# Reordering the two router passages of a two-layer transformer kernel: shift logits, first expert weights, placements

## The chip, the cores and the metric

The kernel runs on one core of one Trainium2 chip, with all operands in fp32 in HBM. The metric is the device time of one execution in microseconds. TensorE's granted clock has two levels, 1.2 and 2.4 GHz; the profile writes them as 0.5 and 1.0.

## The reference, cut to what matters

Two layers run over 256 context rows and 256 latent rows of 1024 columns. Layer 0 mixes by grouped-query attention, layer 1 by an S5 scan with a gated linear unit (GLU) behind it. After each mixer comes a mixture of 32 experts in 4 groups. Layer 1 needs the latent rows alone.

```
m = split(silu(c) @ mod_w[i] + mod_b[i], 6)                # shift, scale, gate for mixer and experts
h = h + m[2] * mixer(modulate(rmsnorm(h, norm1_g), m[0], m[1]))
t = modulate(rmsnorm(h, norm2_g), m[3], m[4])              # = rmsnorm(h) * g * (1 + scale) + shift
g_logits = t @ w_group + b_group                           # 4 groups: the largest is taken
e_logits = (t @ w_router + b_router)[of that group]        # 8 experts: the best two are taken
y = sum over e of combine[:, e] * ((silu(t @ w_gate[e]) * (t @ w_up[e])) @ w_down[e])
h = h + m[5] * y
```

## The kernel before

The program order of each engine is written out by hand: the functions are generators, and the order in which they are stepped is the order of the instructions on every engine. An engine works its instructions off in that order, so one that waits holds up all that stand behind it.

**Layer 0's passage.** `attention` ends with `out(t)` for four row tiles: 16 steps of the output projection (L445), then a multiplication and an addition on VectorE (L449, L450). Between these steps TensorE also computes layer 1's modulation, one half of a 1024-column chunk at a time (`mod.half`, L142), and the router's preparation `prep(n, j)` of the tiles that are ready. The modulation weights (24 MB in loads of 1 MB) go through a ring of slots; a slot is loaded again once TensorE has read it. The ring is set by `c.use`: two slots of `own` (buffers named ring) and the five of `new` (buffers named more), while four slots of `own` hold the output projection. The last chunk's modulation stands behind `attention`, in `beside`.

**The router.** For a tile of 128 rows `prep` scales the rows (L647), takes the sum of squares, transposes them (L657), copies the result out of PSUM (L660, L662) and computes the logits (L691). The shift's share of the logits is the same for all rows of one kind and is made by `base(j)` once for each kind: on VectorE shift times router weights (L623), a sum (L625), then one small matmul (L629) and the bias (L631). `base` needs the router's weights `wr`, which `tables` loads on GpSimd's queue. `route` takes the groups and experts (L711 to L723), the exponentials for the combine weights (L726 to L728), the position of each row in its expert's list by a matmul (L732), and writes rows and weights into the lists by matmuls with one-hot matrices (`place`, L776).

**The experts.** In layer 0, `start` computes the row indices, gathers 128 rows for two experts at a time by indirect DMA (L909), and issues weights on GpSimd's queue; the loop `experts` transposes the gathered rows (L923), computes gate and up (L936), transposes (L947), multiplies by the down matrix (L957), and adds into the rows (L1001) two experts later. Expert e+4's weights take the slots of older ones. In layer 1 the rows of an expert are picked by one-hot matmuls (`open`, L859, for the first four experts; `quad`, L823, for the rest).

**Layer 1's passage.** `s5.glu(1, wg)` is the second column half of the GLU, 32 steps of three matmuls (L1825) with tails on VectorE (L1833 to L1841); `EARLY` says after which step which of `prep(0)`, `prep(1)` and `opening` takes one step. Behind the GLU the sequence "121111" and the rest of all generators follow, then `experts`. The GLU's weights are split into two parts (`wsplit`, L1793, L1794) on ScalarE with VectorE or GpSimd.

Of the kernel before, what the change touches and what calls it, by code (L numbers as in the profile page):

```python
# [14 lines left out]
AF = mybir.ActivationFunctionType  # L15
# [510 lines left out]
class Moe:  # L526
# [42 lines left out]
    def tables(self):  # L569

        nc, a, i, nt = self.c.nc, self.c.a, self.layer, self.nt
        nc.gpsimd.memset(self.wr, 0.0)
        nc.gpsimd.dma_start(self.wr[:, :, 0:4], a["moe_w_group"][i].rearrange("(k p) n -> p k n", p=128))
        nc.gpsimd.dma_start(self.wr[:, :, 8:40], a["moe_w_router"][i].rearrange("(k p) n -> p k n", p=128))
        nc.gpsimd.memset(self.br, -BIG)
        nc.gpsimd.dma_start(self.br[:, 0:4], a["moe_b_group"][i:i + 1].to_broadcast([128, 4]))
        nc.gpsimd.dma_start(self.br[:, 8:40], a["moe_b_router"][i:i + 1].to_broadcast([128, 32]))

        nc.gpsimd.iota(self.slot, pattern=[[0, 2], [1, W]], base=int(FAR), channel_multiplier=0,
                       allow_small_or_imprecise_dtypes=True)  # L580
        nc.gpsimd.iota(self.token, pattern=[[1, 128 * nt]], base=0, channel_multiplier=0,
                       allow_small_or_imprecise_dtypes=True)
        nc.gpsimd.iota(self.tok, pattern=[[128, nt]], base=1, channel_multiplier=1, allow_small_or_imprecise_dtypes=True)
# [49 lines left out]
    def prep(self, n, j):  # L633
# [7 lines left out]
        yield  # L641
        if j not in self.lb:
            yield from self.base(j)
        tT = wk.tile([128, KT, 128], F32, name="tT", tag="t4", bufs=T4)
        for f in range(2):
            s = slice(512 * f, 512 * f + 512)
            nc.vector.tensor_mul(t[:, s], h[:, s], scale[:, s])  # L647
            sq = wk.tile([128, 512], BF, name="sq", tag="sq")
            nc.scalar.activation(sq, h[:, s], AF.Square, accum_out=st[:, f:f + 1])
            if f:  # L650
                nc.vector.tensor_add(st[:, 2:3], st[:, 0:1], st[:, 1:2])
                rstd(c, st[:, 3:4], st[:, 2:3], D)
            yield
            yield from self.wait(0, 1)
            p = self.bank("xt")
            for k in range(4):
                nc.tensor.transpose(p[:, 128 * k:128 * k + 128], t[:, 512 * f + 128 * k:512 * f + 128 * k + 128], c.ident)  # L657
            x, p = tT[:, 4 * f:4 * f + 4, :], p.rearrange("p (k n) -> p k n", k=4)
            if f:
                nc.vector.tensor_copy(x, p)  # L660
            else:
                nc.scalar.activation(x, p, AF.Copy)  # L662
                yield
        r = st[:, 3:4]
# [17 lines left out]
        else:  # L682
# [4 lines left out]
            if n + 1 < self.nt:  # L687
                yield
        p = self.bank("gu")
        for k in range(KT):  # L690
# [6 lines left out]
    def route(self, n, L):  # L697
# [25 lines left out]
        V.tensor_tensor(self.ob[:, n], oh[:, 0], oh[:, 1], op=OP.add)  # L723
        V.tensor_scalar(ngm, gm[:, 0:1], -1.0, None, op0=OP.mult)
        V.tensor_scalar(nm, em[:, 0:1], -1.0, None, op0=OP.mult)
        A.activation(gx, L[:, 0:4], AF.Exp, bias=ngm, accum_out=gs)  # L726
        A.activation(ex, xe, AF.Exp, bias=nm, accum_out=es)
        A.activation(m, em[:, 0:2], AF.Exp, bias=nm)  # L728
        yield from self.wait(2, 4)
# [6 lines left out]
        if n + 1 == self.nt:  # L736
            next(self.opening)
        V.tensor_reduce(self.pe[:, n], x, axis=AX.X, op=OP.add)
        rhs = self.rhs[:, n]
        for k in range(2):  # L740
            V.tensor_scalar(rhs[:, k, 0:32], oh[:, k], self.tok[:, n:n + 1], None, op0=OP.mult)
        hots = self.hots(self.pe[:, n])
        yield from self.wait(0, 3)
        self.place(n, hots, [rhs[:, k, 0:32] for k in range(2)], slice(0, 32))
        if self.xg is not None and n + 1 == self.nt:
            self.start()
        yield from self.wait(1, 0)
        V.reciprocal(gw, gs)
        V.reciprocal(es, es)
# [4 lines left out]
        for k in range(2):  # L754
            V.tensor_scalar(rhs[:, k, 32:64], oh[:, k], m[:, k:k + 1], None, op0=OP.mult)
        yield from self.wait(0, 3)
        self.place(n, hots, [rhs[:, k, 32:64] for k in range(2)], slice(32, 64))
# [13 lines left out]
    def place(self, n, hots, rhs, s):  # L771

        if n == 0 and s.start == 0:
            self.acc = self.bank("ht")
        for k in range(2):
            self.c.nc.tensor.matmul(self.acc[:, s], hots[k], rhs[k], start=(n + k == 0 and s.start == 0),  # L776
                                    stop=(n == self.nt - 1 and k == 1), skip_group_check=True)
# [48 lines left out]
    def start(self):  # L826

        self.indices()
        c = self.c
        c.queue = c.nc.gpsimd  # L830
        self.gather(0)
        self.gather(1)
        self.first[1] = self.weights(1)
        self.gather(2)
        for e in (2, 3):
            self.first[e] = self.weights(e)
        c.queue = c.nc.sync
# [186 lines left out]

    def experts(self, extra, rows, last):

# [7 lines left out]
        else:  # L1034
            self.pairs(self.slots())
            g = [self.onehot_tile("r") for _ in range(2)]
# [5 lines left out]
        for e in range(NE + 1):  # L1042
            if e < NE:
# [15 lines left out]
                for k, _ in enumerate(self.hidden(xT, *wt[e][:2])):  # L1059
                    if e and k == 0:  # L1060
                        hT = self.turn_hidden(hid)
                    for _ in range((2, 4)[k] if end else 2):
                        next(pieces, None)
# [117 lines left out]

EARLY = {4: 0, 8: 0, 10: 0, 12: 0, 13: 1, 14: 1, 17: 0, 18: 1, 20: 0, 25: 0, 26: 0, 28: 0, 30: 0, 31: 2}

# [664 lines left out]
def build(tc, a, dbg=()):  # L1848
    with ExitStack() as ctx:
# [17 lines left out]
        with ExitStack() as part:  # L1867
# [5 lines left out]
            def tail():  # L1873
# [8 lines left out]
                for ch in range(6):  # L1882
                    mod.load(1, ch)
                c.use(*own, *new)
                return box[0]
# [7 lines left out]
            moe.more(*pools(part, "exp"))  # L1893
            moe.ahead(1)
            beside = chain(*(mod.steps(1, ch, range(4 * h, 4 * h + 4)) for ch, h in halves))
            while prep:
                for g in list(prep):
                    if next(g, g) is g:
                        prep.remove(g)
# [37 lines left out]
        with ExitStack() as right:  # L1937
            with ExitStack() as left:
# [17 lines left out]
                early.close()  # L1956
                moe = Moe(c, 1, ((2, 0), (3, 0)), *pools(right, "moe1", "right"))
                c.use(s5.own[2], s5.own[4], *s5.own[5:9])
                gp = left.enter_context(tc.tile_pool(name="glu2", bufs=1, reuse_waits="tile"))
                wsplit(gp, 0, 0, nc.gpsimd)  # L1960
                wsplit(gp, 0, 1, nc.vector)
                moe.tables()
                prep = [moe.prep(n, j) for n, (_, j) in enumerate(moe.tiles_j)]
# [11 lines left out]
            moe.ahead(5)  # L1975
            for n in map(int, "121111"):
                next((*prep, moe.opening)[n])
            for _ in chain(moe.opening, *prep):
                pass
# [9 lines left out]

            moe.experts(iter(()), iter(()), last)  # L1990

# [43 lines left out]
```

## Time and profile before

| | |
|---|---|
| median of 3 runs | 1171.84 us (1169.45 to 1175.91) |
| the profiled execution | 1171.68 us, its span 1169.7 us |
| busy: TensorE, VectorE, ScalarE, GpSimd | 1005.0, 734.3, 330.7, 141.5 us |
| mean granted clock of TensorE | 0.945 |
| HBM read, mean over the span | 313.77 MB, 286 GB/s |

The span is the time from the first to the last instruction; 2.0 us of the execution lie around it. The attention's output projection runs from 279 to 378 us, layer 0's experts from 400 us, layer 1's second GLU half from 836 to 878 us, its experts from 895 us to the end.

### The profile page before, as it was taken

To read this page: it belongs to the slowest core of one execution; us is meant where nothing else is said; L and a number is where in the kernel's file an instruction comes from. 1 tells how busy PE (TensorE), PEld (TensorE's weight loads), DVE (VectorE), ACT (ScalarE), POOL (GpSimd) and SP (SyncE) were. 2 spreads that over 40 slices of the span, in tenths; PEclk is the share of its full clock that TensorE was granted. 3 is DMA by queue.
4 is the path that set the end of the run, shared out by engine and by line. 5 is a ranking of instruction groups with operands and counts; after the bars stand their busy time and mean duration, and the time that the engine had idled before them with its cause. 6 is when DMAs were issued, how large, how long until landed. Compare 5 with 4: busy or idle time off the path is not lost. (4 is left out here: it accounts for less than half of the span.)

```text
span 1169.7 us, 17609 instructions
## 1 busy us (share of the span) xinstructions
PE 1005.0 (86%) x6645; PEld 567.7 (49%) x6645; DVE 734.3 (63%) x1812; ACT 330.7 (28%) x735; POOL 141.5 (12%) x214
## 2 busy tenths in 40 slices
PE   2798889879799779999989976579777999999996
PEld 1443444444354435555544432455566555555553
DVE  7679888992355314455888977499954444434444
ACT  3332334343011122111221212784422222222220
POOL 2211121124110400000000002012400000000000
PEclk9999999999899789999998988889978999999999
DMA  9944854855993999999876845999938899999941
GB/s 301 330 156 158 284 203 149 278 200 188 357 334 141 340 413 372 395 385 346 342 311 225 325 178 161 201 259 328 364 122 350 340 385 371 382 374 378 381 201 37
DMA packets 88360, 331.77 MB, mean 284 GB/s; under 512 B 10168, under 2 KB 19096, under 8 KB 69840
## 3 DMA queue, kind: packets, MB, share of 16 engines
q1 hardware_dynamic: 67616, 283.76, 66.7%
q0 software_dynamic: 9232, 25.73, 6.4%
q10 hardware_dynamic: 11424, 21.12, 5.1%
q8 instruction: 54, 0.88, 0.3%
q14 instruction: 34, 0.28, 0.1%
HBM read 313.77 MB, written 20.99 MB: 286 GB/s over the span
## 5 line engine op out<-in xcount | busy, mean ns | idle before, releaser
L936 PE MATMUL gu<-ring,xq 128*64 128x256 f32 x1056 | 146.3, 392 | 1.4 <-DVE sl L941 1.4
L936 PE MATMUL gu<-more,xq 128*64 128x256 f32 x992 | 140.0, 391 | 6.1 <-DMA more<-moe_w_up 5.3
L1001 PE MATMUL co<-yh,oT 128*128 128x512 f32 x188 | 89.2, 474 | 26.7 <-DVE z L992 8.4
L936 PEld LDWEIGHTS gu<-ring,xq 128*64 128x64 f32 x1056 | 82.6, 141 | 60.7 <-issue 25.6
L936 PEld LDWEIGHTS gu<-more,xq 128*64 128x64 f32 x992 | 78.0, 140 | 60.9 <-issue 25.7
L352 PE MATMUL acc<-ring,uT 128*128 128x512 f32 x192 | 94.6, 626 | 2.9 <-ACT uT L328 2.9
L940 ACT ACTIVATE sl<-gu 64x256 f32<-64x256 f32 x64 | 24.1, 377 | 248.5 <-PE gu L936 248.5
L1009 DVE TENSOR_TENSOR sum<-sum,co 128x512 f32<-128x512 f32 x92 | 59.6, 683 | 33.6 <-PE co L1001 33.4
L1001 PE MATMUL co<-yl,oT 128*128 128x512 f32 x188 | 79.1, 421 | 0.3 <-DVE yl L986 0.3
L949 DVE COPY hT<-ht 128x128 f32<-128x128 f32 x64 | 18.4, 288 | 92.6 <-PE ht L947 92.5
L957 PE MATMUL y<-ring,hT 128*64 128x512 f32 x272 | 69.8, 636 | 0.4 <-DVE hT L949 0.4
L941 DVE TENSOR_TENSOR sl<-gu,sl 64x256 f32<-64x256 f32 x64 | 27.3, 427 | 64.4 <-ACT sl L940 63.2
L1001 PEld LDWEIGHTS co<-yh,oT 128*128 128x128 f32 x188 | 36.6, 195 | 61.7 <-issue 18.5
L957 PE MATMUL y<-more,hT 128*64 128x512 f32 x240 | 58.0, 604 | 0.4 <-DVE hT L949 0.4
L352 PEld LDWEIGHTS acc<-ring,uT 128*128 128x128 f32 x192 | 35.4, 199 | 38.1 <-issue 33.6
L142 PE MATMUL gv<-ring,cT 128*32 128x256 f32 x512 | 35.8, 421 | 17.8 <-DMA ring<-mod_w 17.8
L1003 DVE TENSOR_TENSOR h<-h,co 128x512 f32<-128x512 f32 x64 | 41.1, 681 | 6.8 <-PE co L1001 6.8
L1001 PEld LDWEIGHTS co<-yl,oT 128*128 128x128 f32 x188 | 37.4, 199 | 7.7 <-DVE yl L986 4.4
L909 POOL DMA_INDIRECT xg<-td,row x16 | 16.2, 1015 | 196.3 <-PE xt L923 193.5
L407 ACT ACTIVATE pr<-sc,mx 128x256 f32<-128x256 f32 (+1 forms) x32 | 18.6, 581 | 73.7 <-DVE mx L406 72.7
L986 DVE SCALAR_TENSOR_TENSOR yl<-z,pt,yh 128x512 fp32r<-128x512 f32 x30 | 22.5, 751 | 25.5 <-ACT yh L985 25.5
L1639 ACT ACTIVATE un<-ut,cols 128x32 f32<-128x32 f32 x128 | 35.3, 412 | 6.3 <-PE ut L1632 6.3
(439 smaller groups left out, 1874.4 us busy)
## 6 DMA issues: line engine op xcount, KB each, us to landing
ring<-mod_w SPq DMA_DIRECT2D x32, 1024.0 KB, 8.1
ring<-moe_w_gate SPq DMA_DIRECT2D x32, 1024.0 KB, 8.0
ring<-moe_w_up SPq DMA_DIRECT2D x32, 1024.0 KB, 7.6
ring<-moe_w_down SPq DMA_DIRECT2D x32, 1024.0 KB, 9.9
more<-moe_w_down SPq DMA_DIRECT2D x29, 1024.0 KB, 10.7
more<-moe_w_gate SPq DMA_DIRECT2D x29, 1024.0 KB, 7.4
more<-moe_w_up SPq DMA_DIRECT2D x29, 1024.0 KB, 9.1
more<-mod_w SPq DMA_DIRECT2D x16, 1024.0 KB, 9.0
```

Of the source, the lines that this page charges most:

```text
L142: nc.tensor.matmul(self.bank[i, b][32 * q:32 * q + 32, o:o + 256], self.cT[:, k, :], self.tiles[i, ch, k // 2][:, k % 2, 256 * q:256 * q + ...
L352: nc.tensor.matmul(acc, uT[:, k, 128 * t:128 * t + 128], wq[b][k // 4][:, k % 4, :], start=(k == 0), stop=(k == KT - 1))
L407: nc.scalar.activation(pr[:, 0:nk], s[:, 0:nk], AF.Exp, bias=mx[:, h, 0:1], accum_out=mx[:, h, 1:2])
L936: nc.tensor.matmul(p[s:s + 64, 0:HID], xT[k], w[k // 4][:, k % 4, :], start=(k == 0), stop=(k == KT - 1), skip_group_check=True)
L940: nc.scalar.activation(sl, p[0:64, 0:HID], AF.Silu)
L941: nc.vector.tensor_tensor(sl, p[64:128, 0:HID], sl, op=OP.mult)
L957: self.c.nc.tensor.matmul(p[o:o + 64, :], hT[:, f, :], wd[f][:, 512 * n:512 * n + 512], start=(f == 0), stop=(f == 1), skip_group_check=True)
L986: nc.vector.scalar_tensor_tensor(lo, y, w, hi.bitcast(F32), op0=OP.mult, op1=OP.subtract)
L1001: nc.tensor.matmul(p, oh[:, 128 * n:128 * n + 128], y, start=(i == 0), stop=(i + 1 == len(rows)))
L1003: nc.vector.tensor_tensor(h, h, p, op=OP.add)
L1009: nc.vector.tensor_tensor(a, a, p, op=OP.add)
L1639: nc.scalar.activation(u4[:, k, s], ut[:, 64 * k + 32 * s:64 * k + 32 * s + 32], AF.Identity, bias=shift, scale=scale)
```

## The change

Six edits. `base` moves from ahead of the transpositions to behind them (and behind layer 0's write of the rows), ahead of the logits that need its result. The last tile's second transposition is copied out by ScalarE, not VectorE. The exponentials move from ahead of the positions to behind the first placement. In layer 0 the ring's order after the modulation is changed so that the first expert's weights go into `new[1:4]` and the second's into `own[2:5]`, both on SyncE's queue (`ahead(2)`); `start` issues one expert's weights, not three; the last two tiles are stepped in reverse order. In layer 1 the router's tables come ahead of the weight split and on SyncE's queue; tile 0's logits and route move from the GLU to behind it, between tile 1's steps (`LAST`); and all placements and exponentials of both tiles move into experts 0 and 1, with their list in PSUM bank `co`, not `ht`. In layer 1 a `wait(1, ...)` is one further step; in layer 0 the numbers of waiting steps stay as they were.

```diff
     def tables(self):
         nc, a, i, nt = self.c.nc, self.c.a, self.layer, self.nt
-        nc.gpsimd.memset(self.wr, 0.0)
-        nc.gpsimd.dma_start(self.wr[:, :, 0:4], a["moe_w_group"][i].rearrange("(k p) n -> p k n", p=128))
-        nc.gpsimd.dma_start(self.wr[:, :, 8:40], a["moe_w_router"][i].rearrange("(k p) n -> p k n", p=128))
+        queue = nc.sync if self.one else nc.gpsimd
+        nc.gpsimd.memset(self.wr[:, :, 4:8], 0.0)
         nc.gpsimd.memset(self.br, -BIG)
-        nc.gpsimd.dma_start(self.br[:, 0:4], a["moe_b_group"][i:i + 1].to_broadcast([128, 4]))
-        nc.gpsimd.dma_start(self.br[:, 8:40], a["moe_b_router"][i:i + 1].to_broadcast([128, 32]))
+        queue.dma_start(self.wr[:, :, 0:4], a["moe_w_group"][i].rearrange("(k p) n -> p k n", p=128))
+        queue.dma_start(self.wr[:, :, 8:40], a["moe_w_router"][i].rearrange("(k p) n -> p k n", p=128))
+        queue.dma_start(self.br[:, 0:4], a["moe_b_group"][i:i + 1].to_broadcast([128, 4]))
+        queue.dma_start(self.br[:, 8:40], a["moe_b_router"][i:i + 1].to_broadcast([128, 32]))
...
         yield
-        if j not in self.lb:
-            yield from self.base(j)
         tT = wk.tile([128, KT, 128], F32, name="tT", tag="t4", bufs=T4)
...
             x, p = tT[:, 4 * f:4 * f + 4, :], p.rearrange("p (k n) -> p k n", k=4)
-            if f:
+            if f and n + 1 < self.nt:
                 nc.vector.tensor_copy(x, p)
...
                 nc.scalar.activation(x, p, AF.Copy)
+            if f == 0:
                 yield
...
                 yield
+        if j not in self.lb:
+            yield from self.base(j)
         p = self.bank("gu")
...
         V.tensor_tensor(self.ob[:, n], oh[:, 0], oh[:, 1], op=OP.add)
-        V.tensor_scalar(ngm, gm[:, 0:1], -1.0, None, op0=OP.mult)
-        V.tensor_scalar(nm, em[:, 0:1], -1.0, None, op0=OP.mult)
-        A.activation(gx, L[:, 0:4], AF.Exp, bias=ngm, accum_out=gs)
-        A.activation(ex, xe, AF.Exp, bias=nm, accum_out=es)
-        A.activation(m, em[:, 0:2], AF.Exp, bias=nm)
         yield from self.wait(2, 4)
...
             next(self.opening)
+        yield from self.wait(1, 0)
         V.tensor_reduce(self.pe[:, n], x, axis=AX.X, op=OP.add)
...
         hots = self.hots(self.pe[:, n])
-        yield from self.wait(0, 3)
+        yield from self.wait(1, 3)
         self.place(n, hots, [rhs[:, k, 0:32] for k in range(2)], slice(0, 32))
...
         yield from self.wait(1, 0)
+        V.tensor_scalar(ngm, gm[:, 0:1], -1.0, None, op0=OP.mult)
+        V.tensor_scalar(nm, em[:, 0:1], -1.0, None, op0=OP.mult)
+        A.activation(gx, L[:, 0:4], AF.Exp, bias=ngm, accum_out=gs)
+        A.activation(ex, xe, AF.Exp, bias=nm, accum_out=es)
+        A.activation(m, em[:, 0:2], AF.Exp, bias=nm)
         V.reciprocal(gw, gs)
...
             V.tensor_scalar(rhs[:, k, 32:64], oh[:, k], m[:, k:k + 1], None, op0=OP.mult)
-        yield from self.wait(0, 3)
+        yield from self.wait(1, 3)
         self.place(n, hots, [rhs[:, k, 32:64] for k in range(2)], slice(32, 64))
     def wait(self, one, more):
...
     def place(self, n, hots, rhs, s):
         if n == 0 and s.start == 0:
-            self.acc = self.bank("ht")
+            self.acc = self.bank("co" if self.one else "ht")
         for k in range(2):
...
         self.gather(1)
-        self.first[1] = self.weights(1)
+        self.first[2] = self.weights(2)
         self.gather(2)
-        for e in (2, 3):
-            self.first[e] = self.weights(e)
         c.queue = c.nc.sync
     def shifts(self):
...
-    def experts(self, extra, rows, last):
+    def experts(self, extra, rows, last, rest=iter(())):
...
         else:
-            self.pairs(self.slots())
             g = [self.onehot_tile("r") for _ in range(2)]
...
                         hT = self.turn_hidden(hid)
+                    for _ in range({0: 1, 2: 2}.get(2 * e + k, 0)):
+                        next(rest, None)
+                    if not direct and e == k == 1:
+                        for _ in rest:
+                            pass
+                        self.pairs(self.slots())
                     for _ in range((2, 4)[k] if end else 2):
...
-EARLY = {4: 0, 8: 0, 10: 0, 12: 0, 13: 1, 14: 1, 17: 0, 18: 1, 20: 0, 25: 0, 26: 0, 28: 0, 30: 0, 31: 2}
+EARLY = {4: 0, 8: 0, 12: 0, 13: 1, 14: 1, 17: 0, 18: 1, 20: 0}
+LAST = "100100221112"
...
                     mod.load(1, ch)
-                c.use(*own, *new)
+
+                c.use(*new[1:4], *own[2:], new[4], *own[:2], new[0])
                 return box[0]
...
             moe.more(*pools(part, "exp"))
-            moe.ahead(1)
+            moe.ahead(2)
             beside = chain(*(mod.steps(1, ch, range(4 * h, 4 * h + 4)) for ch, h in halves))
             while prep:
-                for g in list(prep):
+                for g in prep[::-1]:
                     if next(g, g) is g:
...
                 moe = Moe(c, 1, ((2, 0), (3, 0)), *pools(right, "moe1", "right"))
+                moe.tables()
                 c.use(s5.own[2], s5.own[4], *s5.own[5:9])
...
                 wsplit(gp, 0, 1, nc.vector)
-                moe.tables()
                 prep = [moe.prep(n, j) for n, (_, j) in enumerate(moe.tiles_j)]
...
             moe.ahead(5)
-            for n in map(int, "121111"):
-                next((*prep, moe.opening)[n])
-            for _ in chain(moe.opening, *prep):
+            for n in map(int, LAST):
+                next((*prep, moe.opening)[n], None)
+            for _ in moe.opening:
                 pass
...
-            moe.experts(iter(()), iter(()), last)
+            moe.experts(iter(()), iter(()), last, turns(*prep))
```

## Rows read from the trace of the kernel before

**Rows 1.** Busy time by stretch: engines with instructions, TensorE's clock, DMA share, GB/s
```profile
412.70:439.26 26.56, 20.44 (x104) 10.37 (x103) 4.37 (x12) 5.26 (x10) 0.99 (x1) 0.81 1.00 408
...
840.00:860.00 20.00, 11.31 (x42) 8.99 (x42) 12.39 (x16) 2.57 (x7) 6.16 (x10) 0.74 0.50 167
```
**Rows 2.** TensorE's longest wait, 896 to 1160 us: us in total, times, longest
```profile
PE co L1001 <- ACT sl L940: 5.7, 13, 0.4
```
**Rows 3.** Timeline of layer 0's tile 0 (start, duration, instructions, [idle before <- releaser])
```profile
300.00 1.98 PE L445 MATMUL acc<-ring,oT 128*128 128x512 f32 x4
...
307.29 0.49 DVE L623 TENSOR_TENSOR lbx<-wr,sr 128x320 f32<-128x320 f32 x1 [8.92 <-DMA wr<-moe_w_router]
...
308.63 0.65 PE L629 MATMUL gu<-L,A 128*128 128x40 f32 x2 [6.65 <-DVE L L625]
...
309.08 3.76 PE L445 MATMUL acc<-ring,oT 128*128 128x512 f32 x4
...
312.77 2.63 PE L142 MATMUL gv<-more,cT 128*32 128x256 f32 x32
```
**Rows 4.** DMA issues of 283 to 294.2 us: median us to landing
```profile
ring<-mod_w SPq DMA_DIRECT2D x1, 1024.0 KB, 16.9
```
**Rows 5.** Timeline from the modulation's last half in attention to layer 0's first expert
```profile
358.75 1.93 PE L142 MATMUL gv<-more,cT 128*32 128x256 f32 x32
...
392.45 1.16 POOL L909 DMA_INDIRECT xg<-td,row  x1 [1.69 <-DVE sc L749]
...
399.78 4.58 PE L936 MATMUL gu<-ring,xq 128*64 128x256 f32 x26
```
**Rows 6.** Timeline of SyncE's queue: the first issue of expert weights
```profile
378.89 0.35 SPq L89 DMA_DIRECT2D ring<-moe_w_gate  x1
```
**Rows 7.** Timeline of TensorE, layer 0's experts 2 to 5
```profile
415.41 2.52 PE L936 MATMUL gu<-more,xq 128*64 128x256 f32 x14 [2.06 <-DMA more<-moe_w_up]
...
428.25 3.67 PE L936 MATMUL gu<-more,xq 128*64 128x256 f32 x14 [3.19 <-DMA more<-moe_w_up]
...
439.26 1.90 PE L936 MATMUL gu<-ring,xq 128*64 128x256 f32 x16
...
447.69 0.60 PE L936 MATMUL gu<-ring,xq 128*64 128x256 f32 x4
```
**Rows 8.** Timeline of layer 1's passage, second GLU half to first expert
```profile
848.10 0.69 DVE L1838 TENSOR_TENSOR h<-h,g 128x512 f32<-128x512 f32 x1
...
851.40 0.62 PE L629 MATMUL gu<-L,A 128*128 128x40 f32 x2 [8.69 <-DVE L L625]
...
854.52 1.05 PE L657 MATMUL xt<-ident,t 128*128 128x128 f32 x4
...
872.53 0.18 PE L732 MATMUL gu<-ob,before 128*128 128x32 bf16 x1 [2.47 <-DVE ob L723]
...
874.64 0.77 PE L1825 MATMUL o<-wh,zz 128*128 128x512 f32 x1
...
878.30 0.39 PE L1825 MATMUL o<-wl,zz 128*128 128x512 f32 x1
...
895.28 4.95 PE L936 MATMUL gu<-ring,xq 128*64 128x256 f32 x32
```
**Rows 9.** Timeline, further durations: logits, combine weights, a placement, a table load
```profile
360.61 0.63 PE L776 MATMUL ht<-rhs,A 128*128 128x32 f32 x4
...
862.48 2.03 PE L691 MATMUL gu<-wr,tT 128*128 128x40 f32 x16
...
872.58 0.30 ACT L726 ACTIVATE gx<-L,sc 128x4 f32<-128x4 f32 x1 [3.22 <-DVE sc L724]
...
873.92 0.15 DVE L748 RECIPROCAL sc<-sc 128x1 f32<-128x1 f32 x1
...
875.23 0.39 DVE L755 TENSOR_SCALAR rhs<-oh,sc 128x32 f32<-128x32 f32 x2
...
892.51 1.28 ACT L940 ACT_TABLE_LOAD   x1
```

## Prediction, made before the changed kernel was run

> **What bounds the kernel now.** I read the page first, then a table of busy time by stretch, the waits of TensorE, and the timelines of the two passages in which the table shows TensorE idle. The page's shares of busy time are averages and hide this: in most of the span TensorE has work without a gap, and the time is lost in a few places. In layer 1's expert loop TensorE's longest kind of wait adds up to 5.7 us and names no DMA [rows 2]: whatever starts that loop earlier ends the kernel earlier by as much. Layer 0 has two losses. First, at 302 us TensorE stands 6.65 us before tile 0's shift logits, because VectorE waits for the router's weights, and afterwards four matmul instructions take 3.76 us where four like them took 1.98 [rows 3]: the clock is at its lower level of 1.2 GHz. Second, experts 2 and 3 take 26.56 us at a DMA share of 1.00 and 408 GB/s [rows 1], with waits of 2.06 and 3.19 us for up weights [rows 7]. Layer 1's passage has one of 8.69 us before the same shift logits, a chain of short ones around 872 us, and 16.6 us between the last GLU matmul and the first expert's [rows 8]; the mean clock in its first 20 us is 0.74 [rows 1].
>
> **Term 1, layer 0's shift logits.** Removed: the idle 6.65, the slow projection 3.76 - 1.98 = 1.8, and a slow modulation half, 2.63 against 1.93 us [rows 3, 5], 0.7; together 9.1 us. After the change TensorE goes from 302 us into transpositions that need only scaled rows. The matmul of `base` comes in step 11 of the projection instead of step 5: six steps later at 0.99 us (two of the four instructions in 1.98 us), two modulation halves at 1.93 and two transpositions, which I put at 0.6 each. That is 5.9 + 3.9 + 1.2 = 11.0 us, so 313 us. The router's weights are there at 307.3 [rows 3], and the two VectorE operations behind them need about 1.3 us: no wait is left. New is that the logits use the PSUM bank of the shift's matmul right behind it and so wait for VectorE's addition. Queued before that on VectorE may be the projection's two operations; I take 1.1 us for both kinds of row, between 0.5 and 2.6. Net -8.0. Late next are the modulation's loads: the one issued at about 293.8 landed 16.9 us later [rows 4], at 310.7, just when the faster TensorE asks for it. Bounds: -4.1 (the idle time alone, less 2.6) to -9.1.
>
> **Term 2, layer 0's last tiles.** The last tile's copy leaves VectorE, where it stood behind the previous tile's reciprocals; but that tile's exponentials and reciprocals now stand between the last tile's logits and its route. The first nearly pays the second back: I take -0.8 up to the gather. From the gather's issue at 392.45 to the first expert's matmul it is 7.3 us [rows 5]; with two experts already loaded the gather meets less traffic, I take -0.7. Exponentials behind `start` delay only the second placement, which is hidden by the gather in flight; uncovered it costs some 1 us. Sum -1.5, bounds +1 to -3.
>
> **Term 3, layer 0's first weights.** Expert 0's first load was issued at 378.89 [rows 6], in a slot that the last modulation chunk had to free. In the new order expert 0 has the slots of chunk 4, which TensorE finishes with its half at 358.75 + 1.93 [rows 5], 18 us earlier; expert 1 has three of the projection's slots, read out at the projection's end. At 408 GB/s [rows 1] a load of 1 MB takes 2.6 us, so the six take 16 us and are there before the first expert starts. SyncE then issues two of expert 3's loads as the last chunk is read, and GpSimd, behind two gathers, expert 2's three: 13 us for five loads, while expert 2 is due 412.70 - 399.78 = 12.9 us after expert 0 [rows 1, 5] and its loads start some 5 us before expert 0 does. So experts 2 and 3 no longer wait. What they then take: expert 4 takes 447.69 - 439.26 = 8.43 us [rows 7]. Two of these are 16.9, a gain of 9.7; expert 2 makes none of the additions that expert 4 makes, so the gain is more, and I take -11. Bounds: -5.2 (the two waits alone, clock unchanged) to -12.
>
> **Term 4, layer 1.** In the GLU TensorE stood from 842.7 to 851.4 [rows 8]. Now it does two more GLU steps and then waits at tile 0's transposition for VectorE's L647, which comes right behind L1838: 848.10 + 0.69 + about 0.7 = 849.5, against 854.52: 5.0 us, not 8.7, because VectorE's queue of weight split and GLU tail is late next. Out of the GLU go tile 0's logits, 2.0 [rows 9]; the stretch from 870.06 (2.47 before 872.53) to 874.64 [rows 8], 4.6; a placement, 0.6 [rows 9]; and some three slow matmul groups behind it (0.77 against 0.39 [rows 8]), 1.2. The clock, which falls in the wait that is left too, costs 1.5 more, since more of the GLU then lies behind it. Sum: the GLU ends 11.9 us earlier. Behind it stood 16.6 us. Out goes tile 1's combine chain with its placement: 875.23 + 0.39 - 873.92 = 1.7 on VectorE, 0.6 on TensorE and their hand-overs, about 3. In come tile 0's logits 2.0, its route on VectorE 2.5 (as 870.06 to 872.53), and 0.5 of waiting for the shift's addition, which stands behind the GLU's tail. That is 18.5 us, +1.9; at full clock +0, at the lower level throughout some +4.
> The moved placements cost time in expert 1: four at 0.6 are 2.5 us. The second ones also wait: two negations, three exponentials at 0.3 and the 1.7 us chain make 2.85 us a tile, 5.7 for both, one behind the other on VectorE; TensorE has meanwhile half an expert, 1.9 [rows 7], and two placements, 1.3, so it waits 2.5. Sum +5.0, bounds +2.5 to +7. Queued behind that wait is the rest of expert 1; nothing on another engine is due before it. The two further table loads, 1.28 us each [rows 9], I count as nothing: the first fits before the negations, the second before expert 1's silu, whose result is due 4 us later; without cover, 2.6. The router's loads on SyncE's queue now stand ahead of the weight split and are wanted only behind tile 0's second transposition, so I count them as nothing too; if they were late, the wait would be what it is now, 8.7 us at most. Net -11.9 + 1.9 + 5.0 = -5.0, bounds -9 to 0.
> The rows show a table load of 1.28 us, and none shows an exponential waiting behind one. The Trainium skill (ScalarE: Activation LUTs, "Table sets: the hidden batching unit" and "What ACT_TABLE_LOAD costs") asks to do all functions of one set together and puts a switch at 2.66 us with the drain; this change puts exponentials between two silus. By it the wait in expert 1 would be about 1 us longer, and the time 1147.
>
> **Sum.** -8.0 - 1.5 - 11 - 5.0 = -25.5 on the span of 1169.7: 1144.2. The execution is 2.0 longer than its span, so 1146; its 1171.7 is the runs' median within 0.2, and nothing is to be corrected.
>
> **Rivals.**
> *Weights still late* (0.16): five loads in flight when expert 2 is due, as GpSimd's stand behind SyncE's; half of term 3's wait stays. For it: DMA already runs at 1.00 [rows 1]. Against: the first six are out of the way. 1146 + 7 = 1153.
> *The modulation loads bind* (0.12): a TensorE that is 8 us earlier meets loads that are not [rows 4]; term 1 shrinks to about 2. 1152.
> *Full clock in layer 1* (0.10): fewer gaps keep it up, net -9. 1142.
> *It doesn't do what it says* (0.07): the slots are free no earlier, because something other than TensorE's reading holds them, and layer 1's placements eat its gain. Terms 1 and 2 stay in part: 1163 to 1170.
> *Slower* (0.05): layer 1's first experts start at the lower clock, and expert 1's wait keeps it there. An expert of 8.4 us [rows 7] then takes 16.8: three experts eat 25.5 us, and with four it is 1146 + 34 = 1180. Against: before, GLU matmuls were fast again (0.39) 4 us after a slow one at 874.64 [rows 8].
>
> **How the numbers follow.** The forecast has 0.50 and its own range is 1142 to 1150. With the first three rivals 0.88 lies between 1140 and 1156; taking the bounds of terms 1 and 4, 1138 to 1158. A measurement of this kernel tells about 0.5%, 6 us: faster 0.90 (all but the last two rivals, and part of the fourth), same 0.06, slower 0.04.
>
> **What would show it.** Right: no wait at L629 in either layer; expert 0's loads issued before the projection's end; no DMA wait in the first four experts, which then take some 28 us; the last GLU matmul to the first expert 17 to 20 us; a wait of 2 to 3 us at L776 in expert 1. Wrong: TensorE waiting for modulation loads, for expert 2, or for VectorE behind the GLU longer than 20 us.

## The result and the profile after

| | before | after |
|---|---|---|
| median of 4 runs, us | 1170.94 (1169.45 to 1175.91) | 1144.27 (1142.39 to 1145.37) |
| ratio, 95% interval | | 0.976 (0.973 to 0.980) |
| span of the profiled execution, us | 1169.7 | 1143.5 |
| mean granted clock | 0.945 | 0.955 |

The kernel became 26.7 us faster by the medians, 26.2 by the profiled spans; 1146 with a span shorter by 25.5 was forecast. In the changed file most functions that the prediction names stand a few lines further on: L629 is L630, L631 is L632, L647 is L646, L691 is L693, L776 is L779, L936 is L937, and layer 1's GLU matmul L1825 is L1832; in the files of the runs further down some stand one or two lines further on again.

To see where the time went, both traces are cut at nine points that both have, by TensorE's rows: (a) the start of a modulation matmul at 292.64 us ahead of layer 0's logits, which the change does not touch, (b) tile 2's position matmul, (c) layer 0's first expert, (d) the transposition of its fifth expert's hidden rows, (e) S5's first transposition, (f) the end of the last GLU matmul, (g) layer 1's first expert, (h) its first combine matmul, (i) the end of the span. The last column says which term of the prediction covers a stretch.

| stretch | before | after | difference | predicted |
|---|---|---|---|---|
| start to a | 292.64 | 294.26 | +1.6 | 0, not touched |
| a to b | 84.09 | 77.31 | -6.8 | -8.0, term 1 |
| b to c | 23.05 | 22.48 | -0.6 | -1.5, term 2 |
| c to d | 49.74 | 37.61 | -12.1 | -11, term 3 |
| d to e | 245.18 | 243.29 | -1.9 | 0 |
| e to f | 183.99 | 170.82 | -13.2 | -11.9, term 4, the GLU |
| f to g | 16.59 | 17.88 | +1.3 | +1.9, term 4, behind the GLU |
| g to h | 22.23 | 26.33 | +4.1 | +5.0, term 4, experts 0 and 1 |
| h to i | 252.19 | 253.52 | +1.3 | 0, not touched |

Layer 0, TensorE's timeline at tile 0, to be read against [rows 3]:

```profile
301.62 1.12 PE L445 MATMUL acc<-ring,oT 128*128 128x512 f32 x2
302.58 0.60 PE L656 MATMUL xt<-ident,t 128*128 128x128 f32 x4
303.01 2.74 PE L445 MATMUL acc<-ring,oT 128*128 128x512 f32 x6
305.69 1.93 PE L142 MATMUL gv<-more,cT 128*32 128x256 f32 x32
307.55 0.66 PE L656 MATMUL xt<-ident,t 128*128 128x128 f32 x4
308.04 3.60 PE L445 MATMUL acc<-ring,oT 128*128 128x512 f32 x8
```

Nothing waits here: the transpositions stand where 6.65 us were lost, and eight projection matmuls take 3.60 us where four took 3.76. But at the logits of tile 0, and of tile 2, whose shift is another one:

```profile
314.47 1.95 PE L693 MATMUL gu<-wr,tT 128*128 128x40 f32 x16 [0.62 <-issue]
...
361.82 0.42 PE L630 MATMUL gu<-L,A 128*128 128x40 f32 x2
363.25 1.98 PE L693 MATMUL gu<-wr,tT 128*128 128x40 f32 x16 [1.02 <-DVE lb L632]
```

Tile 2's logits wait 1.02 us for the addition, and the mean clock of the 7 us from 364 us on is 0.76 (first row of windows below). Tile 0's stand idle for 0.62 us; the profile names no releaser, but they start 0.1 us after the end of the same addition on VectorE. SyncE's issues of weights, layer 0:

```profile
347.59 0.35 SPq L89 DMA_DIRECT2D more<-moe_w_gate  x1
...
353.54 0.38 SPq L89 DMA_DIRECT2D more<-moe_w_down  x1
361.04 0.33 SPq L89 DMA_DIRECT2D ring<-moe_w_gate  x1
...
369.61 0.38 SPq L89 DMA_DIRECT2D ring<-moe_w_down  x1
379.20 0.33 SPq L89 DMA_DIRECT2D ring<-moe_w_gate  x1
```

Expert 0's first load is issued at 347.59 instead of 378.89 [rows 6], expert 1's three between 361 and 370. Windows (columns as in [rows 1]) of the stretch behind tile 2's logits, of layer 0's first four experts, of the one behind the GLU and of layer 1's first experts:

```profile
364.00:371.00 7.00, 7.00 (x25) 3.81 (x24) 2.88 (x14) 0.60 (x1) 0.00 (x0) 0.76 0.76 274
394.05:421.40 27.35, 27.03 (x188) 15.01 (x189) 5.42 (x15) 8.98 (x16) 3.55 (x6) 0.96 0.95 365
845.77:863.65 17.88, 12.63 (x74) 11.91 (x73) 11.47 (x42) 4.18 (x7) 1.17 (x2) 0.71 0.99 391
878.00:890.00 12.00, 12.00 (x79) 5.81 (x75) 3.06 (x10) 2.24 (x5) 0.00 (x0) 0.87 0.72 275
```

Four experts take 27.35 us, 399.78 to 439.26 before [rows 5, 7]; experts 2 and 3 alone took 26.56 [rows 1]. Layer 1, TensorE's timeline:

```profile
829.47 1.08 PE L656 MATMUL xt<-ident,t 128*128 128x128 f32 x4 [5.48 <-DVE t L646]
...
845.60 0.31 PE L630 MATMUL gu<-L,A 128*128 128x40 f32 x2
848.71 0.53 PE L693 MATMUL gu<-wr,tT 128*128 128x40 f32 x3 [2.80 <-DVE lb L632]
...
875.76 0.63 PE L779 MATMUL co<-rhs,A 128*128 128x32 f32 x4 [1.70 <-DVE rhs L758]
```

The 8.69 us [rows 8] have become 5.48, two GLU steps later; 2.80 us are lost to the addition behind the GLU, and 1.70 in expert 1.

### The profile page after: what moved, and what is told of

It reads as the page before. It is cut to its first block, busy times and chain, and to the rows that moved or that the text cites. A ratio compares the mean times of both kernels' runs of the same rounds, so it can differ in the third digit from the quotient of the medians.

```text
span 1143.5 us, 17608 instructions
## 1 busy us (share of the span) xinstructions
PE 993.5 (87%) x6645; PEld 562.8 (49%) x6645; DVE 733.5 (64%) x1810; ACT 333.3 (29%) x738; POOL 133.5 (12%) x204
## 5 line engine op out<-in xcount | busy, mean ns | idle before, releaser
L937 PE MATMUL gu<-ring,xq 128*64 128x256 f32 x1024 | 151.0, 384 | 3.5 <-DVE sl L942 3.4
L937 PE MATMUL gu<-more,xq 128*64 128x256 f32 x1024 | 153.4, 390 | 0.0
L937 PEld LDWEIGHTS gu<-more,xq 128*64 128x64 f32 x1024 | 86.0, 140 | 56.6 <-issue 24.8
L937 PEld LDWEIGHTS gu<-ring,xq 128*64 128x64 f32 x1024 | 84.4, 137 | 57.3 <-issue 19.5
L942 DVE TENSOR_TENSOR sl<-gu,sl 64x256 f32<-64x256 f32 x64 | 27.3, 427 | 56.2 <-ACT sl L941 54.9
```

The lines of the kernel that those rows point to most:

```text
L937: nc.tensor.matmul(p[s:s + 64, 0:HID], xT[k], w[k // 4][:, k % 4, :], start=(k == 0), stop=(k == KT - 1), skip_group_check=True)
L942: nc.vector.tensor_tensor(sl, p[64:128, 0:HID], sl, op=OP.mult)
```

## The experiments

Each run was timed beside the kernel before on the same chip, so ratios are to before and compare with 0.976. The sizes come from the stretches of the table above, because the untouched stretches differ between executions by more than the effects (last section). Each stretch is that of one profiled execution.

**The changed kernel once more, beside the last three runs.** 

> The changed kernel once more, beside the three that follow, to compare them on one chip and to see which stretches differ between two executions of one kernel. Theory: 0.976 of the kernel before; its stretches from the projection to the first expert, from there to the fifth, the GLU, and from it to the first expert are within 0.5 us of the first execution's (13.1, 27.4, and 17.9 us), and what differs is the stretches in which VectorE and TensorE work short of each other, by the clock. Rival: the stretches that the change touched differ by 2 us or more themselves, so that a gain of 2 us in one execution says nothing.

Measured: 0.974 (0.971 to 0.977), median 1145.11. The six touched stretches are 77.33, 22.43, 37.71, 170.84, 17.88 and 26.32 us: within 0.1 us of the first execution. Start to a took 291.81 against 294.26. The theory holds: here a stretch tells tenths of a microsecond where the whole time does not tell 2 us. That has limits. In other kernels whose code for a stretch is that of the changed one, a to b also took 76.6 us (two of them), c to d up to 38.9, and g to h 24.75 (four), each time because the clock fell, or came back, at another moment.

**Layer 0's weights as before.**
```diff
-                c.use(*new[1:4], *own[2:], new[4], *own[:2], new[0])
+                c.use(*own, *new)
-            moe.ahead(2)
+            moe.ahead(1)
```
with `start` issuing experts 1, 2 and 3 again. 

> Layer 0's first weights as before the change (the six attention slots first, one expert asked for ahead, experts 1, 2 and 3 by GpSimd behind the gathers); everything else as changed. Theory, that the slots and the order of the loads are what term 3 gained: experts 0 to 3 take 39 to 41 us again in place of 27.4, TensorE waits two or three times for an up weight, 5 us or more together, and the clock falls behind the waits; the time is 1144.3 + 12 = 1156, between 1154 and 1159. Rival, that the faster layer 0 in front of it is what helped the loads: no more than 2 us of waits for weights, 1149 or less.

Measured: 0.986 (0.981 to 0.991); c to d 52.62 us, 15.0 more than after, and TensorE's waits there

```profile
PE gu L939 <- DMA more<-moe_w_up: 6.4, 2, 4.3
...
PE gu L939 <- DMA more<-moe_w_gate: 2.5, 2, 1.6
```

The theory holds, with sizes somewhat above the expected ones: the first four experts took 42.4 us, the whole 1159.72. Before, this stretch was 12.1 us longer than after; undoing the edit costs 2.9 more than that, because the waits for weights add up to 8.9 us here and to 6.2 before. Why they are longer was not followed up.

**The slots alone, and the order of the loads alone.** The first undoes only these two, the second only the line with `c.use`:
```diff
-            moe.ahead(2)
+            moe.ahead(1)
...
-        self.first[2] = self.weights(2)
+        self.first[1] = self.weights(1)
         self.gather(2)
+        for e in (2, 3):
+            self.first[e] = self.weights(e)
```


> The new order of the slots is kept, but only expert 0 is asked for ahead, and GpSimd issues the loads of experts 1, 2 and 3 behind the gathers, as before the change. Theory, that early free slots are what counts: expert 0 is there early, nine loads of 1 MB are left at the gathers, 9 x 2.6 = 23.4 us from 387 us, which just meet expert 3 at 413; at most one wait of 1 to 2 us, time 1144 to 1148. Rival, that what counts is that the loads are issued before the gathers: experts 1 to 3 wait 4 us or more together and the clock falls, 1150 to 1156.

> The counterpart of the run with the slots alone: two experts are asked for ahead of the gathers and GpSimd issues expert 2's loads alone, as changed, but the slots are in their old order, the projection's six first. Theory, that it counts that six loads are issued ahead of the gathers: expert 0's and 1's loads are issued at 373 to 381 us, expert 2 waits at most once for about 2 us, from the first expert's start to the fifth's 30 us or less (27.35 as changed, 42 with both undone). Rival, that neither alone helps and early slots are needed too: 36 us or more, with waits of 4 us or more for the weights of experts 1 to 3.

| b to d, us | old order of loads | new order |
|---|---|---|
| old slots | 74.84 | 68.89 |
| new slots | 71.49 | 60.09 |

Measured: 0.986 (0.980 to 0.992) for the slots alone, 0.980 (0.978 to 0.982) for the order alone; the kernel with both old is the run before this one. My theory for the slots alone fell: with expert 0 early, nine loads issued behind the gathers do not arrive in time, and TensorE waits 4.7 us for up weights, which is what the rival says; the time, 1158.5, is above both expected ranges. The order alone is worth 6.0 us, the slots alone 3.4, both 14.8: each lets the other work. The first expert to the fifth took 31.5 us with the order alone, between the two expectations, and the wait was not where either put it. TensorE's waits of the kernel with the order alone:

```profile
PE xt L924 <- DMA xg<-td,row: 5.8, 2, 5.5
...
PE y L958 <- DVE hT L950: 2.4, 1, 2.4
```

Of the eight loads issued at 371 to 381 us the second landed at 383.0, but the fourth to sixth only at 388.2, 392.2 and 397.3: they are in flight when the gather starts at 384. It takes 8.6 us to land (4.4 after the change), and its rows come 5.5 us after TensorE is ready for them (1.2 after the change). That early slots let the loads finish ahead of the gather, and that this is what spares it, fits both; it was not tried by itself.

**Layer 0's base ahead of the transpositions.**
```diff
         yield
+        if j not in self.lb and not self.one:
+            yield from self.base(j)
         tT = wk.tile([128, KT, 128], F32, name="tT", tag="t4", bufs=T4)
```


> In layer 0 alone the shift's part of the logits is made ahead of the transpositions again. Theory, that term 1 is the wait for the router's weights and the lower clock behind it: TensorE waits 5 to 7 us at L630 near 305 us and the four projection matmul instructions behind it take about 3.8 us; in return the wait of 1.0 us for the addition at 363 us and the fall of the clock behind it, 2 us together, are gone; +7, 1151. Rival, that the shorter fill of the weights' tile brings the router's weights earlier, so that nothing waits: +2 or less, 1144 to 1146.

Measured: 0.981 (0.976 to 0.986). The wait is back, with the slow matmuls behind it:

```profile
315.44 0.65 PE L630 MATMUL gu<-L,A 128*128 128x40 f32 x2 [6.55 <-DVE L L626]
315.88 3.76 PE L445 MATMUL acc<-ring,oT 128*128 128x512 f32 x4
```

a to b is 83.36 us, 6.0 more than after. VectorE again waits for the router's weights, 8.83 us, so the theory holds. The whole time does not tell the size: the four runs go from 1149.85 to 1157.40, and in the profiled one, the longest, start to a took 299.54 us.

**Layer 0's last tiles as before.**
```diff
-                for g in prep[::-1]:
+                for g in list(prep):
...
-            if f and n + 1 < self.nt:
+            if f:
                 nc.vector.tensor_copy(x, p)
```


> Layer 0's last tiles as before the change in two points: the tiles take their steps in the order of their numbers, and the last tile's second half is copied by VectorE; the exponentials stay behind. Theory, that the copy stood behind the previous tile's chain: from the tile-2 position matmul to the last tile's it is 2 us longer than 9.4 us as changed, and layer 0's first expert 2 us later. Rival, that VectorE's chain is as long in either order: within 0.5 us.

Measured: 0.979 (0.976 to 0.982); b to c 23.26 us against 22.48 and 22.43: 0.8 us, nearer the rival. TensorE waits 1.99 us for the copy, as expected, but with the change it waits 1.69 us a little later, for the route of the same tile: VectorE's chain takes its place. Behind c this execution lost another 2.4 us, 1.3 of it in the first expert's 32 gate and up matmuls (6.07 us for 4.78) at a lower clock. The kernel with the addition ahead in both layers, which leaves these tiles as changed, took 5.63 us there too, so this is not shown to come from the edit.

**Layer 1 as before,** layer 0 as changed; the core of the edit:
```diff
+        if j not in self.lb and self.one:
+            yield from self.base(j)
...
-            for n in map(int, LAST):
-                next((*prep, moe.opening)[n], None)
-            for _ in moe.opening:
+            for n in map(int, "121111"):
+                next((*prep, moe.opening)[n])
+            for _ in chain(moe.opening, *prep):
```


> Layer 1 as before the change (router's loads on GpSimd's queue behind the split, shift's logits ahead of the transpositions, tile 0's logits, route and placement in the GLU, the other placement in the head, none among the experts), layer 0 as changed. Theory, the trace's own account of term 4: GLU 12.9 us longer, 1.3 less behind it, 4.1 less in experts 0 and 1: 7.5, 1152. Rival, that the GLU's gain is the early router's loads and the rest costs as much as it gains: the stretch behind the GLU and the first two experts give back 10 us or more, 1147 or less.

Measured: 0.981 (0.979 to 0.983). The wait at L630 is 8.91 us, e to f 180.85 (10.0 more than after), f to g 22.29 (4.4 more), g to h 22.39 (3.9 less); together +10.5, not +7.5. It is not quite before's layer 1: the order of steps inside the route is shared with layer 0 and stays changed, so both tiles' exponentials and chains stand ahead of the first expert. That fits the 4.4: TensorE waits 2.47 and 1.35 us there for the combine operands. The rival falls; the head gives back nothing.

**Layer 1's placements in the head.**
```diff
-            for _ in moe.opening:
+            for _ in chain(moe.opening, *prep):
...
-            moe.experts(iter(()), iter(()), last, turns(*prep))
+            moe.experts(iter(()), iter(()), last)
```


> Layer 1's placements are made ahead of expert 0 again, all four behind the gather's matmuls; the rest as changed. Theory, that expert 1 is the cheaper place: the 1.7 us wait in expert 1 and the four placements there, 4.1 us together, are gone, but expert 0 starts only when VectorE has made both tiles' position and combine operands, which took 2.1 + 5.1 us behind 865 us, so it starts 9 to 10 us after now; net +5 to +6, 1150. Rival, that the move only shifted the cost, since the chain of one tile (1.7) and its placement (0.6) are all that stood in the head: expert 0 starts 3 us later, net -1, 1143.

Measured: 0.981 (0.976 to 0.987). TensorE ahead of the first expert:

```profile
862.38 0.60 PE L779 MATMUL co<-rhs,A 128*128 128x32 f32 x4 [1.62 <-DVE A L771]
865.25 1.92 PE L779 MATMUL co<-rhs,A 128*128 128x32 f32 x8 [2.27 <-DVE rhs L758]
868.51 1.06 PE L779 MATMUL co<-rhs,A 128*128 128x32 f32 x4 [1.34 <-DVE rhs L758]
```

f to g is 26.69 us (+8.8), g to h 23.50 (-2.8): +6.0 as expected. The experts are the cheaper place.

**The exponentials half an expert earlier.**
```diff
-                    for _ in range({0: 1, 2: 2}.get(2 * e + k, 0)):
+                    for _ in range({0: 1, 1: 2}.get(2 * e + k, 0)):
```


> Layer 1's first placements and the exponentials with their chain are put half an expert earlier, into expert 0's second half; the second placements stay in expert 1. Theory, that the 1.7 us wait in expert 1 is VectorE's two chains not being done: it is gone, and from the first expert to the first combine matmul it is 24.6 us, 26.3 as changed. Rival, that ScalarE's table loads between the exponentials and the silus are the price: expert 0's or 1's silu comes 1 to 2 us late, TensorE waits for it at the transposition of the hidden rows, and the stretch stays at 26 us or more.

Measured: 0.975 (0.973 to 0.977); g to h 28.22 us, 1.9 worse. The 1.7 us wait is gone, and one of 3.16 us for VectorE's product with expert 0's silu is new. ScalarE:

```profile
867.45 1.28 ACT L748 ACT_TABLE_LOAD   x1
...
872.25 0.30 ACT L748 ACTIVATE gx<-L,sc 128x4 f32<-128x4 f32 x1 [1.59 <-DVE sc L746]
...
873.15 1.28 ACT L941 ACT_TABLE_LOAD   x1
874.44 0.38 ACT L941 ACTIVATE sl<-gu 64x256 f32<-64x256 f32 x1
```

My theory fell and the rival holds: silu stands behind both tiles' exponentials, which VectorE's two chains keep apart, and behind the second table load. In the changed kernel the silu that stands there is due later, and no TensorE wait names it. The Trainium skill (ScalarE: Activation LUTs, "Table sets: the hidden batching unit") asks to keep one set's functions together; the runs agree where the next silu is on the path, and show no loss where it is not. The 2.66 us a switch that the prediction took from it, and the 1 us of waiting by that figure, did not show: the load takes 1.28 us here and the silu starts at its end, at 874.44, and in the changed kernel the wait in expert 1 was 1.7 us, not 3.5.

**Layer 1's router loads on GpSimd's queue.**
```diff
-        queue = nc.sync if self.one else nc.gpsimd
+        queue = nc.gpsimd
```


> Layer 1's router loads are on GpSimd's queue, still ahead of the weight split, instead of SyncE's. Theory, as the prediction counted them, at nothing: the GLU and the stretch behind it are within 1 us of the changed kernel's. Rival: four issues of 0.6 to 0.9 us and their waits stand ahead of GpSimd's half of the weight split, on which TensorE waits in the GLU: 3 us or more longer there.

Measured: 0.976 (0.973 to 0.979), median 1149.69 beside 1145.11; e to f 173.98 us, 3.2 more than after, f to g 0.2 less. My theory fell and the rival holds: TensorE waits 2.2 us in all for GpSimd's half of the weight split, which is at 825.7 us here and 3.8 us later in its stretch than after the change. Ahead of it on GpSimd stand the four issues and a wait of 3.36 us. That the loads cost nothing in the changed kernel is due to SyncE's queue.

**The addition ahead of the logits,** in layer 1, and then in both layers.
```diff
         if j not in self.lb:
             yield from self.base(j)
+            yield
...
-EARLY = {4: 0, 8: 0, 12: 0, 13: 1, 14: 1, 17: 0, 18: 1, 20: 0}
+EARLY = {4: 0, 8: 0, 12: 0, 13: 1, 14: 1, 17: 0, 18: 1, 20: 0, 27: 0}
```


> In layer 1 the matmul of the shift's logits and VectorE's addition are put behind the GLU's 28th step, four steps ahead of tile 0's logits, so that the addition stands ahead of the GLU's last two VectorE operations and the second tile's scaling. Theory, that the wait of 2.8 us at tile 0's logits is that addition's place in VectorE's queue: the wait is 0.5 us or less, and the last GLU matmul to the first expert's is 15 to 16 us, 17.9 as changed. Rival, that VectorE is the bound there whatever the order: the second tile's transposition waits in its place for its scaling, 17.4 us or more.

> The addition for the shift's logits is made a step ahead of the logits in both layers. Theory: in layer 0 the wait of 1.0 us at tile 2's logits and the lower clock behind it (2 us together) go, in layer 1 3 us go behind the GLU as in the run before; 5 us less than the changed kernel on the same chip, some 0.4%. Rival: the step that is put in between only moves tile 0's and tile 2's later work in layer 0, and the last tile's chain with it: layer 0's first expert starts no earlier, 3 us less in all or nothing that can be told.

Measured: 0.974 (0.971 to 0.976) and 0.967 (0.965 to 0.970). On the chip of the second, its median is 1137.65 (1136.40 to 1138.11) and the changed kernel's 1145.11 (1142.51 to 1148.42): it beats both kernels, by 7.5 us against the expected 5. The first cannot be told from the changed kernel by its time. TensorE in layer 0 with the addition ahead:

```profile
359.23 0.41 PE L630 MATMUL gu<-L,A 128*128 128x40 f32 x2
359.48 1.10 PE L445 MATMUL acc<-ring,oT 128*128 128x512 f32 x2
360.67 1.98 PE L694 MATMUL gu<-wr,tT 128*128 128x40 f32 x16
362.47 1.96 PE L445 MATMUL acc<-ring,oT 128*128 128x512 f32 x4
```

No wait, the projection at full speed, and a to b 73.93 us, 3.4 less than after. Laid side by side matmul by matmul, the two traces part in two places: 0.8 us at tile 0's logits, whose 0.62 us of idle time are gone too, and 2.6 at tile 2's, 0.9 of waiting and 1.6 of the lower clock behind it. In layer 1 the wait shrinks to 0.15 us and f to g to 14.67 us in both kernels, 3.2 less, as the theory for layer 1 has it. But e to f is 2.8 us longer in both (173.67 and 173.61). Of that, 1.9 and 1.6 were there when tile 0's transposition started, ahead of the first instruction that the edit moves; in the one, the clock had fallen 96 us behind e, where eight matmuls took 5.62 us at 0.50 instead of 3.60 at 1.00; in the other, ScalarE had waited 2.41 us for a GLU weight's load. The remaining 1.0 and 1.2 are the base matmul, 0.31, and slower GLU matmuls. So layer 1's net gain is between 0.4 and 2.3 us. Two different causes, both ahead of the edit, speak for chance; one execution of each kernel does not show it.

## Why the prediction was right

The mechanisms were those foreseen, each of terms 1, 3 and 4 has its run, and the errors of the terms nearly cancel (-25.5 predicted, -27.3 in the six touched stretches; with the three others it is -26.2). That the sum came within 0.7 us is in part luck: single terms missed by 0.9 to 2.8 us in both directions, and the stretches put at 0 moved by 1.3 to 1.9 us each.

*Term 1*, -8.0: -6.8. The idle time and the slow projection went as worked out, and no modulation load was waited for. Mis-sized was the 1.1 us for the addition, and its upper bound of 2.6: the two waits were 0.6 and 1.0 us, but with the clock that fell behind them they cost 3.4. Part of that was paid by a gain that was not counted: with the addition ahead, the stretch is 10.2 us shorter than before, not 9.1, and a wait of 0.9 us at a later tile's transposition is among what is gone.

*Term 2*, -1.5: -0.6. The part up to the gather was -0.6, near the -0.8. The 0.7 from the gather to the first expert was not there: 7.33 us before and 7.34 after (386.71 to 394.05). The run with the old slots shows that loads in flight do delay a gather, by more than 4 us (8.6 us to landing, against 4.4 both before and after); less traffic just did not help this one. What the last tiles' edits do is shown as a whole, not one by one.

*Term 3*, -11: -12.1, and no wait for weights. The prediction gave the gain to slots and order without splitting it; each alone is worth less than half. A further 1.9 us came in d to e, where neither trace waits for a weight. They arise 161 to 208 us behind d, and TensorE's mean clock from 160 to 210 us behind d was 0.86 before and 0.97 after. The four kernels with the old slots or the old order take 244.8 to 245.3 us for the stretch and seven executions of the others 243.3 to 243.4; three took 243.6 to 244.35, so what it hangs on is not settled.

*Term 4*, -5.0: -7.8. Tile 0's transposition starts 5.3 us earlier behind e (5.0 predicted), the rest of the GLU gave 7.9 (6.9 predicted). Behind the GLU +1.3 for +1.9; the 0.5 us of waiting for the addition was 2.8, and the rest was shorter than worked out. Experts 0 and 1 +4.1 for +5.0: the wait was 1.7 instead of 2.5, short of the 2 to 3 us named as a sign; the first expert's 32 gate and up matmuls took 3.67 us for 4.95 before [rows 8], which was not counted. And 1.6 of the 4.1 is a clock that falls behind that wait in some executions and not in others: eight down matmuls take 3.47 us or 1.94, and g to h is 26.3 us in six of the executions that are alike there and 24.75 in four, the ones with the addition ahead among them. The two table loads cost nothing, as counted; half an expert earlier they would not have been free.

None of the rivals came: no weights late, no modulation load waited for, and behind the GLU the clock stays at 0.71 without eating the experts.

## What to carry to other kernels

Cut the trace at starts that both kernels share and compare stretches: most repeat to a tenth of a microsecond where whole times differ by 5 us and more, and those that do not can be followed matmul by matmul to where the clock fell. A short wait for another engine is to be priced with the clock behind it; here 1.0 us at tile 2 cost 2.6, 1.6 us of waiting in all cost 3.4, and one step of distance between a matmul, its addition and the reader of the result gave it back. Early buffers and early issues are one edit: either alone gave less than half.

## What was not expected of the hardware

**The clock falls in stretches that are the same.** TensorE waits 3.0 us for ScalarE at 231 us in both kernels; windows before, and then after:

```profile
230.00:235.00 5.00, 1.90 (x8) 1.23 (x9) 4.77 (x17) 2.21 (x8) 2.08 (x4) 1.00 0.91 334
235.00:240.00 5.00, 4.65 (x49) 2.31 (x47) 4.93 (x18) 2.60 (x7) 0.00 (x0) 1.00 0.28 99
```
```profile
230.00:235.00 5.00, 1.99 (x7) 1.30 (x8) 4.80 (x17) 2.12 (x7) 2.07 (x4) 0.75 0.87 325
235.00:240.00 5.00, 5.00 (x18) 2.77 (x16) 3.30 (x13) 1.76 (x5) 0.00 (x0) 0.57 0.29 103
```

The clock fell in one and not in the other, and that is the +1.6 from the start to a. In all 14 profiled executions the wait is 3.0 us; from its end to the next modulation matmul it is 4.19 us in two of them, before and the one with the addition ahead in both layers, and 5.16 to 6.44 in the others. The whole stretch from the start to a takes 290.9 to 299.7 us, with no instruction of TensorE changed in it. The last eight matmuls of the kernel took 3.89 us before and 5.58 after, again with no instruction changed, which is more than the +1.3 from h to i; over the 14 it is 3.9 in three and 5.4 to 5.6 in eleven.

**VectorE stands still beside GpSimd.** Layer 1's weight split after the change, GpSimd and then VectorE:

```profile
816.30 5.62 POOL L1801 TENSOR_TENSOR wl<-ring,wh 128x1024 fp32r<-128x1024 f32 x2 [2.35 <-ACT wh L1800]
```
```profile
816.16 0.69 DVE L1848 TENSOR_TENSOR h<-h,g 128x512 f32<-128x512 f32 x1
816.77 0.68 DVE L1847 TENSOR_TENSOR g<-o,g 128x512 f32<-128x512 f32 x1
817.48 2.19 DVE L1848 TENSOR_TENSOR h<-h,g 128x512 f32<-128x512 f32 x1
819.60 4.54 DVE L1801 TENSOR_TENSOR wl<-ring,wh 128x1024 fp32r<-128x1024 f32 x2
```

An addition of 0.69 us takes 2.19, and two subtractions that take 2.35 in the run with the addition ahead in layer 1 take 4.54: 3.7 us of VectorE, just ahead of the scaled rows for which TensorE waits 5.48 us. The change did not make this: before, the same instructions take 2.19 and 4.55. In the run named, two additions take 2.88 and 2.17 instead, so the loss is as large there. L1847 in between, which reads one operand from PSUM, is not slowed. The Trainium skill (SBUF — State Buffer, "Who interferes with whom") says that a VectorE instruction with two SBUF inputs contends with a GpSimd instruction that reads SBUF, and that the pair of ports they share is an exclusive lock. The trace agrees: the 2.19 us end at 819.67, 0.6 us after the first of GpSimd's two instructions, half of the 5.62 us, is over, as if the addition's 0.69 us began only then.
